# Seven block products in another order, with their weight sums spread over the row

## The chip, the core and the metric

One NeuronCore of a Trainium2 chip. TensorE (PE) multiplies into PSUM banks, VectorE (DVE) and ScalarE (ACT) work beside it, GpSimd (POOL) does next to nothing here, and SyncE (SP) issues the transfers from HBM. Each engine works through its own list of instructions in the order in which they stand, and engines wait for each other by semaphores. The metric is the time of one execution on the device in microseconds.

## The reference, cut to what matters

A decoder layer over 256 tokens of width 2048: a mixer (attention and a convolution), then a gated feed-forward of width 5632. The change lies in the feed-forward:

```python
h = rmsnorm(x, norm_pre_ffn[l])
g = jnp.einsum('bsd,df->bsf', h, w_gate[l])
up = jnp.einsum('bsd,df->bsf', h, w_up[l])
f = jnp.einsum('bsf,fd->bsd', jax.nn.silu(g) * up, w_down[l])
x = x + rmsnorm(f, norm_post_ffn[l])
```

## The kernel before, in words

**fp32 out of three products.** An fp32 operand is split into a rounded part h and a remainder l. A weight tile holds 4 x 128 rows and 512 columns (128 partitions x 2048 numbers, 1 MB). Its `split` is one cast on ScalarE (`wh`, L185 or L915) and one subtraction on VectorE (`wl`, L186 or L916). TensorE then makes 12 matmuls of 512 columns with it for 128 tokens: 8 with `wh`, then 4 with `wl`. These 12 matmuls are a **step**.

**A pair.** The 5632 columns are done 512 at a time, f = 0 to 10. For f = 1 to 10 the gate and the up product of one f are a `Pair`. With X = [X11 X12; X21 X22] (two token blocks, the upper half of the 2048 inputs in two blocks) and W = [r11 r12; r21 r22] (gate columns, up columns) the upper half of the inputs is done with seven block products, P1 to P7, in place of eight. The lower half is done plainly: g0 and g1 are its two gate tiles, u0 and u1 its two up tiles, each with a step for either token block (a and b). That makes 7 + 8 = 15 steps to a pair. P1, P2 and P3 take r11, r21 and r22 as they are; P5, P7, P6 and P4 take sums of weights: r11 becomes r12 - r11, r12 becomes r22 - r12, x becomes r22 - r11, and later x becomes r21 - x (`last_sum`). Each of these is one VectorE instruction over 128 x 2048 (L946). The left operands (`sumh`, `suml`) are sums of blocks of X, formed once by `form_sums`.

**What is collected.** P1, P6, P5 and P3 run in bank b1, P2, g0a and g1a in b2, P7, g0b, g1b and P4 in b7, u1b ends in b8. ScalarE copies b1 away after P1, P6 (`v`) and P5 (`s`, L1016); VectorE adds b7 to s (L1017, the "s add"). `gate(0)` after g1a and `gate(1)` after P4 add v to the bank on VectorE (L1000), then ScalarE takes the silu (L1001). `up(0)` after u0's and u1's steps for block a, and `up(1)` for block b (L1026 and L1005), multiply the two; then `act_put` has TensorE transpose the result (`ft`, eight matmuls), and ScalarE and VectorE split it (L208, L209). The buffers M that hold v, s and sg are three in turn, so the s of one pair is written where `up(1)` of the pair before has read.

**The order.** `steps` lists the steps of a pair; the u steps of a pair are put between the first steps of the next one (`fill`). `run_stream` goes through the list: after the last step of tile i it splits tile i + 4 and runs what hangs on that tile's `post`. Three buffers "w" take the loads; a load is issued when VectorE has read what the buffer held. Jobs that `spawn` puts aside run so many steps later. Each engine gets its instructions in the order in which the Python code makes them.

**The stages.** After f = 0 come parts of the feed-forward: f = 1, 2, then the down product; f = 3 to 5, down; 6 to 8, down; 9 and 10, down. A pair follows directly on another pair six times (f = 2, 4, 5, 7, 8, 10); I call that a **transition**, and count it from P7 of one pair to P7 of the next.

Of the kernel before, what the change touches and what calls it, by code (L numbers as in the profile page):

```python
# [25 lines left out]
F32 = mybir.dt.float32  # L26
# [5 lines left out]
P = 128  # L32
# [28 lines left out]
def hybrid_layer_kernel(ctx: ExitStack, tc: tile.TileContext, x, xt, pack, lamv,  # L61
# [664 lines left out]
    def form_sums():  # L726

        r = v3(T("sums"), 4)
        h, l = H2.part(1)
        for tb in range(2):  # L730
            tok = slice(tb * P, (tb + 1) * P)

            nc.vector.tensor_tensor(out=r[:, 2 * tb:2 * tb + 2].rearrange("p a (k t) -> p (a k) t", k=4),
                                    in0=h[:, :, tok].bitcast(F32), in1=l[:, :, tok].bitcast(F32),
                                    op=ALU.add)
        for o, a, b, op in [(3, 2, 3, ALU.add), (2, 0, 2, ALU.subtract), (0, 3, 0, ALU.subtract),
                            (1, 1, 0, ALU.subtract)]:
            nc.vector.tensor_tensor(out=r[:, o], in0=r[:, a], in1=r[:, b], op=op)
        sh, sl = v3(T("sumh", F32R), 4), v3(T("suml", F32R), 4)
        nc.scalar.copy(sh, r)  # L740
        nc.vector.tensor_tensor(out=sl, in0=r, in1=sh.bitcast(F32), op=ALU.subtract)
        st_["S"] = [t.rearrange("p s (k t) -> p s k t", k=4) for t in (sh, sl)]

    def residual(tb, bank):
        xr, mg = st_["x", tb], st_["mixg", tb]
        tok = slice(tb * P, (tb + 1) * P)
        square_into(bank, part[:, tb, 3:4])
        if tb:
            yield 1
        nc.vector.tensor_tensor(out=mg[:, 3 * C:], in0=bank, in1=st_["gpost"][:, 3 * C:],  # L750
                                op=ALU.mult)
        r = partial_rstd(part, tb, "rpost")

        def x2(n):
            c = slice(n * C, (n + 1) * C)
            nc.vector.scalar_tensor_tensor(out=xr[:, c], in0=mg[:, c], scalar=r[:, 0:1],
                                           in1=xr[:, c], op0=ALU.mult, op1=ALU.add)

        def tr(n):
            bk = aux_bank("ht")  # L760
            for j in range(4):
                nc.tensor.transpose(bk[:, j * P:(j + 1) * P],
                                    xr[:, n * C + j * P:n * C + (j + 1) * P], ident)
            for eng in range(2):
                for j in range(4):
                    k = n * 4 + j
                    g = pk[:, PK_GFFN + k:PK_GFFN + k + 1]
                    h, l = H2.at(k, 1, tok)
                    b = bk[:, j * P:(j + 1) * P]
                    if eng == 0:  # L770
                        nc.scalar.activation(h[:, 0], b, ACTF.Copy, scale=g)
                    else:
                        nc.vector.scalar_tensor_tensor(out=l[:, 0], in0=b, scalar=g,
                                                       in1=h[:, 0].bitcast(F32), op0=ALU.mult,
                                                       op1=ALU.subtract)

        x2(0)
        yield 1
        x2(1)
        x2(2)  # L780
        yield 1
        x2(3)
        tr(0)
        for n in range(1, 4):
            yield 1
            tr(n)
        yield 3
        for n in range(4):
            square_into(xr[:, n * C:(n + 1) * C], part2[:, tb, n:n + 1])
        yield 1  # L790
        rstd2[tb] = partial_rstd(part2, tb, "rffn")

        nc.sync.dma_start(xd[tb], xr)
        st_["x", tb] = None
        if tb:
            yield 2
            form_sums()

    oc = []
    need = {0: [lambda: st_["av", 0]], 4: [lambda: st_["av", 1]],  # L800
# [120 lines left out]
    class Pair:  # L921
# [5 lines left out]
        def __init__(self, f, A, k):  # L927
            self.f, self.A, self.k = f, A, k
            cols = [(f * C, C)]
            gt = [WTile(w_gate, 4 * i * P, SPLIT, cols) for i in range(4)]  # L930
            ut = [WTile(w_up, 4 * i * P, SPLIT, cols) for i in range(4)]
            self.g, self.u = gt[:2], ut[:2]
            self.r11, self.r21, self.r12, self.r22 = gt[2], gt[3], ut[2], ut[3]
            self.x = Slot()
            p = self.p = {
                1: Product(self, 1, self.r11, None, [("w", self.r11)]),
                7: Product(self, 7, self.r12, "r", [("r", self.r12), ("r", self.r22)]),
                6: Product(self, 6, self.x),
                5: Product(self, 5, self.r11, "w", [("w", self.x)]),
                2: Product(self, 2, self.r21, None, [("r", self.r21)]),  # L940
                3: Product(self, 3, self.r22, "r"),
                4: Product(self, 4, self.x, "w")}
            p[3].post = [self.last_sum]

        def sub(self, out, a, b):
            nc.vector.tensor_tensor(out=out.w, in0=a.w, in1=b.w, op=ALU.subtract)  # L946

        def sums(self):
            self.sub(self.r11, self.r12, self.r11)
            self.sub(self.r12, self.r22, self.r12)  # L950
            self.sub(self.x, self.r22, self.r11)

        def last_sum(self):
            self.sub(self.x, self.r21, self.x)
# [1 line left out]

        def steps(self, fill):

            fill[0][0][1].post = [self.sums]
            s = {n: [(self, t, n, 0)] for n, t in self.p.items()}  # L960
            g = [[(self, t, f"g{i}", tb) for tb in range(2)] for i, t in enumerate(self.g)]
            return (s[1] + fill[0] + s[7] + s[6] + fill[1] + s[5] + s[2] + g[0] + s[3] + g[1] + s[4])

        def up_steps(self):
            return [[(self, t, f"u{i}", tb) for tb in range(2)] for i, t in enumerate(self.u)]
# [1 line left out]
        def matmuls(self, t, what, tb):  # L967
            tok = [slice(0, P), slice(P, 2 * P)]
            if what == 1:
                self.b1 = mm_bank("b1")  # L970
            elif what == 2:
                self.b2 = mm_bank("b2")
            elif what == 7:
                self.b7 = ps.tile([P, 2, C], F32, tag="sc", bufs=1, name="b7")[:, 0]
            elif what == "u0" and tb == 1:
                self.b8 = mm_bank("b8")
            if what in (1, 2, 4):
# [20 lines left out]

        def gate(self, tb, bank, part):
            nc.vector.tensor_tensor(out=self.sg[:, tb], in0=bank, in1=part, op=ALU.add)  # L1000
            nc.scalar.activation(self.sg[:, tb], self.sg[:, tb], ACTF.Silu,  # L1001
                                 scale=rstd2[tb][:, 0:1])

# [4 lines left out]
        def after(self, what, tb):  # L1008
# [8 lines left out]
                nc.vector.tensor_tensor(out=self.s, in0=self.b7, in1=self.s, op=ALU.add)  # L1017
            elif what == "g1" and tb == 0:
                self.sg = v3(M("sg"), 2)
                self.gate(0, self.b2, self.v[:, 0])  # L1020
            elif what == 4:
                self.gate(1, self.b7, self.v[:, 1])
            elif what == "u1" and tb == 0:
                self.up(0, self.b1)
            elif what == "u1":
                nc.vector.tensor_tensor(out=self.s, in0=self.b8, in1=self.s, op=ALU.add)  # L1026
                self.up(1, self.s)
                st_["act", self.f] = spawn(act_put(self.A, self.k, self.sg), 2)

    def act_put(A, k, sg):  # L1030
        for tb in range(2):
# [138 lines left out]
```

## Time and profile before

| | |
|---|---|
| median of 3 runs | 1110.38 us (1110.32 to 1110.83) |
| the profiled execution's own time | 1110.2 us |
| its span, first to last instruction | 1108.4 us |
| PE busy | 1058.8 us (96%), 4766 matmuls |
| DVE busy | 821.9 us (74%), 858 instructions |
| ACT busy | 561.9 us (51%), 586 instructions |
| granted TensorE clock, mean | 0.990 of full speed |
| HBM | 208.99 MB read, 192 GB/s over the span |

The profiled execution lies 1.8 us above its span (launch and end) and 0.2 us below the median, so its own stretches can be used as they stand. Busy shares are means over stages of different kinds; what a stage waits for is read from that stage. A matmul is drawn to its modelled end, so that matmuls back to back overlap in the rows; the distance of their starts is what each costs.

### The profile page before, as it was taken

The page shows a single profiled execution, that of the slowest core. Times are in us where ns is not written, and L with a number is a line of the kernel's source. Part 1 is how long each engine was busy: PE and PEld are TensorE (multiplying, and loading weights), DVE is VectorE, ACT ScalarE, POOL GpSimd, SP SyncE. Part 2 cuts the span into 40 slices and gives each one's busy share as a digit, 9 for nine tenths or more (in the row PEclk, how much of TensorE's full clock was granted, in tenths as well). Part 3 has the DMA queues.
Part 4 walks back from the last instruction along what each step waited for, and adds up shares of the span by engine and source line. Part 5 has one row for each costly group of instructions (what it writes and reads, how often), then busy time and mean ns, then how long its engine had stood idle before and what let it go on. Part 6 is the DMA issues. An engine that isn't in the chain of part 4 may idle for free.

```text
span 1108.4 us, 12013 instructions
## 1 busy us (share of the span) xinstructions
PE 1058.8 (96%) x4766; PEld 864.7 (78%) x4766; DVE 821.9 (74%) x858; ACT 561.9 (51%) x586; POOL 10.8 (1%) x16
## 2 busy tenths in 40 slices
PE   9999999999999969899999989999999899999996
PEld 7778888788888857688887777888777788887785
DVE  6689999897557788864677867658787865777765
ACT  6754554655636553644454454435374543445541
POOL 0000000001000000000000000000000000000000
PEclk9999999999999989999999999999999999999998
DMA  9876545444848426377372826844553686372661
GB/s 311 302 254 208 190 152 190 152 154 150 304 158 297 153 81 223 114 268 272 106 237 88 283 77 201 299 145 148 193 196 108 214 284 224 88 254 86 243 241 76
DMA packets 114264, 213.97 MB, mean 193 GB/s; under 512 B 4088, under 2 KB 23840, under 8 KB 112928
## 3 DMA queue, kind: packets, MB, share of 16 engines
q1 hardware_dynamic: 114208, 213.21, 56.6%
q8 instruction: 37, 0.61, 0.2%
q14 instruction: 19, 0.16, 0.0%
HBM read 208.99 MB, written 4.21 MB: 192 GB/s over the span
## 4 chain that ended last, share of the span: by engine, by line
PE 63%; DVE 15%; DMA 8%; ACT 7%; issue 6%; POOL 1%; SPq 0%; DVEq 0%; POOLq 0%; ACTq 0%
PE mm L259 15%; PE mm L260 15%; PE mm L262 14%; PE b L993 10%; PE b L996 5%; DVE wl L186 5%; ACT wh L185 4%; DMA w<-in_w_up_dram 3%; DVE w L946 3%; DMA w<-in_w_gate_dram 2%; DVE raw L946 1%; ACT wh L915 1%; DMA w<-in_w_in_dram 1%; DVE wl L916 1%; DVE sg L1005 1%
## 5 line engine op out<-in xcount | busy, mean ns | idle before, releaser
L186 DVE TENSOR_TENSOR wl<-w,wh 128x2048 fp32r<-128x2048 f32 (+1 forms) x160 | 340.0, 2128 | 171.6 <-ACT wh L185 165.6
L185 ACT CAST wh<-w 128x2048 fp32r<-128x2048 f32 (+1 forms) x160 | 284.1, 1781 | 168.4 <-PE mm L260 80.6
L993 PE MATMUL b<-wh,h2h 128*128 128x512 f32 x440 | 172.9, 393 | 9.2 <-DVE s L1017 9.2
L996 PE MATMUL b<-wh,h2l 128*128 128x512 f32 x440 | 171.4, 390 | 0.0
L259 PE MATMUL mm<-wh,act 128*128 128x512 f32 x352 | 137.4, 390 | 0.2 <-ACT act L208 0.2
L260 PE MATMUL mm<-wh,act 128*128 128x512 f32 x352 | 137.1, 389 | 0.2 <-DVE act L209 0.2
L259 PE MATMUL mm<-wh,xh 128*128 128x512 f32 x320 | 127.8, 399 | 0.6 <-ACT wh L185 0.6
L260 PE MATMUL mm<-wh,xl 128*128 128x512 f32 x320 | 125.1, 391 | 0.0
L993 PE MATMUL b<-wl,h2h 128*128 128x512 f32 x440 | 117.7, 389 | 0.0
L916 DVE TENSOR_TENSOR wl<-w,wh 128x2048 fp32r<-128x2048 f32 x40 | 91.2, 2286 | 31.9 <-ACT wh L915 31.9
L993 PEld LDWEIGHTS b<-wh,h2h 128*128 128x128 f32 x440 | 82.6, 188 | 29.3 <-DVE s L1017 11.7
L993 PEld LDWEIGHTS b<-wl,h2h 128*128 128x128 f32 x440 | 82.6, 188 | 17.3
L996 PEld LDWEIGHTS b<-wh,h2l 128*128 128x128 f32 x440 | 82.7, 188 | 16.8
L915 ACT CAST wh<-w 128x2048 fp32r<-128x2048 f32 x40 | 76.4, 1909 | 35.6 <-PE mm L260 15.8
L262 PE MATMUL mm<-wl,act 128*128 128x512 f32 x352 | 94.2, 389 | 0.0
L442 DVE SCALAR_TENSOR_TENSOR conv_acc<-conv_in,pk,conv_acc 128x255 f32<-128x255 f32 (+14 forms) x240 | 94.1, 460 | 0.0
L262 PE MATMUL mm<-wl,xh 128*128 128x512 f32 x320 | 87.3, 391 | 0.2 <-DVE wl L186 0.2
L916 DVE TENSOR_TENSOR wl<-raw,wh 128x2048 fp32r<-128x2048 f32 x30 | 68.6, 2287 | 23.7 <-ACT wh L915 23.7
L993 PE MATMUL b<-wh,sumh 128*128 128x512 f32 x160 | 65.6, 410 | 18.8 <-DVE sg L1000 12.0
L260 PEld LDWEIGHTS mm<-wh,act 128*128 128x128 f32 x352 | 66.1, 188 | 14.1 <-DVE act L209 0.5
L259 PEld LDWEIGHTS mm<-wh,act 128*128 128x128 f32 x352 | 66.1, 188 | 14.1 <-ACT act L208 0.5
L262 PEld LDWEIGHTS mm<-wl,act 128*128 128x128 f32 x352 | 66.1, 188 | 13.7
(170 smaller groups left out, 1290.4 us busy)
## 6 DMA issues: line engine op xcount, KB each, us to landing
w<-in_w_down_dram SPq DMA_DIRECT2D x44, 1024.0 KB, 5.2
w<-in_w_gate_dram SPq DMA_DIRECT2D x34, 1024.0 KB, 5.3
w<-in_w_in_dram SPq DMA_DIRECT2D x24, 1024.0 KB, 5.1
w<-in_w_up_dram SPq DMA_DIRECT2D x24, 1024.0 KB, 5.3
raw<-in_w_up_dram SPq DMA_DIRECT2D x20, 1024.0 KB, 7.7
w<-in_w_out_dram SPq DMA_DIRECT2D x16, 1024.0 KB, 5.0
w<-in_w_in_dram SPq DMA_DIRECT2D x24, 512.0 KB, 5.0
raw<-in_w_gate_dram SPq DMA_DIRECT2D x10, 1024.0 KB, 7.7
```

The costliest lines, as they stand in the source:

```text
L185: nc.scalar.copy(self.h[:, a:b], self.w[:, a:b])
L186: nc.vector.tensor_tensor(out=self.l[:, a:b], in0=self.w[:, a:b], in1=self.h[:, a:b].bitcast(F32), op=ALU.subtract)
L259: nc.tensor.matmul(bank, lhsT=h, rhs=t.h[:, j], start=first, stop=False)
L260: nc.tensor.matmul(bank, lhsT=l, rhs=t.h[:, j], start=False, stop=False)
L262: nc.tensor.matmul(bank, lhsT=h, rhs=t.l[:, j], start=False, stop=last)
L442: return lambda: nc.vector.scalar_tensor_tensor(out=conv_acc[:, cb, s:], in0=conv_in[:, cb, :S - s], scalar=w, in1=conv_acc[:, cb, s:], op ...
L915: nc.scalar.copy(self.h, w)
L916: nc.vector.tensor_tensor(out=self.l, in0=w, in1=self.h.bitcast(F32), op=ALU.subtract)
L946: nc.vector.tensor_tensor(out=out.w, in0=a.w, in1=b.w, op=ALU.subtract)
L993: nc.tensor.matmul(bank, lhsT=h[:, j], rhs=rhs, start=start and pas == 0 and j == 0, stop=stop and pas == 1 and j == SPLIT - 1, skip_group ...
L996: nc.tensor.matmul(bank, lhsT=l[:, j], rhs=rhs, start=False, stop=False, skip_group_check=True)
L1005: nc.vector.scalar_tensor_tensor(out=self.sg[:, tb], in0=src, scalar=rstd2[tb][:, 0:1], in1=self.sg[:, tb], op0=ALU.mult, op1=ALU.mult)
```

## The change: what it does

- The order of a pair's last steps: P5, P2, g0, P3, g1, P4 becomes P5, P2, P3, g0, g1, P4.
- The three weight sums, made together before (after u0's split of the coming pair), are made one each after the splits of P1, u0 and P7.
- b7 was allocated anew for each pair in the first half of a two-bank tile. Now that tile is allocated once, and pairs use its halves in turn. The program as built still holds a wait of P7's first matmul for `gate(1)` of the pair before, though that reads the other half.
- The silu of `gate` is issued two steps after its addition, and `act_put` three steps after `up(1)` in place of two.
- `form_sums` is issued a step earlier, and its split (`split_sums`) two steps after that.

No instruction is added or left out.

```diff
@@ -736,6 +736,9 @@
         for o, a, b, op in [(3, 2, 3, ALU.add), (2, 0, 2, ALU.subtract), (0, 3, 0, ALU.subtract),
                             (1, 1, 0, ALU.subtract)]:
             nc.vector.tensor_tensor(out=r[:, o], in0=r[:, a], in1=r[:, b], op=op)
+        return r
+
+    def split_sums(r):
         sh, sl = v3(T("sumh", F32R), 4), v3(T("suml", F32R), 4)
         nc.scalar.copy(sh, r)
         nc.vector.tensor_tensor(out=sl, in0=r, in1=sh.bitcast(F32), op=ALU.subtract)
@@ -793,8 +796,10 @@
         nc.sync.dma_start(xd[tb], xr)
         st_["x", tb] = None
         if tb:
+            yield 1
+            r = form_sums()
             yield 2
-            form_sums()
+            split_sums(r)
 
     oc = []
     need = {0: [lambda: st_["av", 0]], 4: [lambda: st_["av", 1]],
@@ -940,15 +945,13 @@
                 2: Product(self, 2, self.r21, None, [("r", self.r21)]),
                 3: Product(self, 3, self.r22, "r"),
                 4: Product(self, 4, self.x, "w")}
+
+            p[1].post = [lambda: self.sub(self.r11, self.r12, self.r11)]
+            p[7].post = [lambda: self.sub(self.x, self.r22, self.r11)]
             p[3].post = [self.last_sum]
 
         def sub(self, out, a, b):
             nc.vector.tensor_tensor(out=out.w, in0=a.w, in1=b.w, op=ALU.subtract)
-
-        def sums(self):
-            self.sub(self.r11, self.r12, self.r11)
-            self.sub(self.r12, self.r22, self.r12)
-            self.sub(self.x, self.r22, self.r11)
 
         def last_sum(self):
             self.sub(self.x, self.r21, self.x)
@@ -956,10 +959,10 @@
 
         def steps(self, fill):
 
-            fill[0][0][1].post = [self.sums]
+            fill[0][0][1].post = [lambda: self.sub(self.r12, self.r22, self.r12)]
             s = {n: [(self, t, n, 0)] for n, t in self.p.items()}
             g = [[(self, t, f"g{i}", tb) for tb in range(2)] for i, t in enumerate(self.g)]
-            return (s[1] + fill[0] + s[7] + s[6] + fill[1] + s[5] + s[2] + g[0] + s[3] + g[1] + s[4])
+            return (s[1] + fill[0] + s[7] + s[6] + fill[1] + s[5] + s[2] + s[3] + g[0] + g[1] + s[4])
 
         def up_steps(self):
             return [[(self, t, f"u{i}", tb) for tb in range(2)] for i, t in enumerate(self.u)]
@@ -971,7 +974,10 @@
             elif what == 2:
                 self.b2 = mm_bank("b2")
             elif what == 7:
-                self.b7 = ps.tile([P, 2, C], F32, tag="sc", bufs=1, name="b7")[:, 0]
+
+                if "b7" not in st_:
+                    st_["b7"] = ps.tile([P, 2, C], F32, tag="sc", bufs=1, name="b7")
+                self.b7 = st_["b7"][:, self.f % 2]
             elif what == "u0" and tb == 1:
                 self.b8 = mm_bank("b8")
             if what in (1, 2, 4):
@@ -998,6 +1004,7 @@
 
         def gate(self, tb, bank, part):
             nc.vector.tensor_tensor(out=self.sg[:, tb], in0=bank, in1=part, op=ALU.add)
+            yield 2
             nc.scalar.activation(self.sg[:, tb], self.sg[:, tb], ACTF.Silu,
                                  scale=rstd2[tb][:, 0:1])
 
@@ -1017,15 +1024,15 @@
                 nc.vector.tensor_tensor(out=self.s, in0=self.b7, in1=self.s, op=ALU.add)
             elif what == "g1" and tb == 0:
                 self.sg = v3(M("sg"), 2)
-                self.gate(0, self.b2, self.v[:, 0])
+                spawn(self.gate(0, self.b2, self.v[:, 0])).run()
             elif what == 4:
-                self.gate(1, self.b7, self.v[:, 1])
+                spawn(self.gate(1, self.b7, self.v[:, 1])).run()
             elif what == "u1" and tb == 0:
                 self.up(0, self.b1)
             elif what == "u1":
                 nc.vector.tensor_tensor(out=self.s, in0=self.b8, in1=self.s, op=ALU.add)
                 self.up(1, self.s)
-                st_["act", self.f] = spawn(act_put(self.A, self.k, self.sg), 2)
+                st_["act", self.f] = spawn(act_put(self.A, self.k, self.sg), 3)
 
     def act_put(A, k, sg):
         for tb in range(2):
```

How it moves instructions, at three places. **VectorE in a transition, the later half** (f = 7 to f = 8), from the split of u1 to the s add. `wl` with L186 are splits of u1 and g0 (g1 has its own further on), `wl` with L916 or L921 those of products, `w<-raw,w` is `last_sum`, the three rows with sg and s are `up(0)` and `up(1)`. Before:

```order
L186 TENSOR_TENSOR wl<-w,wh 128x2048
L916 TENSOR_TENSOR wl<-w,wh 128x2048
L916 TENSOR_TENSOR wl<-raw,wh 128x2048
L186 TENSOR_TENSOR wl<-w,wh 128x2048
L1005 SCALAR_TENSOR_TENSOR sg<-b_5527,rffn_2927,sg 128x512
L1026 TENSOR_TENSOR s<-b_5838,s 128x512
L1005 SCALAR_TENSOR_TENSOR sg<-s,rffn_3054,sg 128x512
L916 TENSOR_TENSOR wl<-raw,wh 128x2048
L946 TENSOR_TENSOR w<-raw,w 128x2048
L1017 TENSOR_TENSOR s<-b_5857,s 128x512
```

These are the splits of u1, P5, P2 and g0, the two ups, the split of P3, `last_sum`, the s add. And now:

```order
L186 TENSOR_TENSOR wl<-w,wh 128x2048
L921 TENSOR_TENSOR wl<-w,wh 128x2048
L921 TENSOR_TENSOR wl<-raw,wh 128x2048 x2
L954 TENSOR_TENSOR w<-raw,w 128x2048
L1012 SCALAR_TENSOR_TENSOR sg<-b_5521,rffn_2927,sg 128x512
L1033 TENSOR_TENSOR s<-b_5832,s 128x512
L1012 SCALAR_TENSOR_TENSOR sg<-s,rffn_3053,sg 128x512
L186 TENSOR_TENSOR wl<-w,wh 128x2048
L1024 TENSOR_TENSOR s<-b_3158,s 128x512
```

The split of P3 and `last_sum` have moved ahead of the ups, and the split of g0 behind them.

**VectorE in a transition, the earlier half** (same pair), from P1's split to `gate(1)`. Rows L946 or L954 are the weight sums, L1000 or L1006 the gates. Before (the first row holds the splits of P4 and P1):

```order
L916 TENSOR_TENSOR wl<-w,wh 128x2048 x2
L186 TENSOR_TENSOR wl<-w,wh 128x2048
L946 TENSOR_TENSOR w<-raw,w 128x2048
L946 TENSOR_TENSOR raw<-raw 128x2048
L946 TENSOR_TENSOR w<-raw,w 128x2048
L1000 TENSOR_TENSOR sg<-b_5672,v 128x512
L916 TENSOR_TENSOR wl<-raw,wh 128x2048
L1000 TENSOR_TENSOR sg<-b_5579,v 128x512
```

And now:

```order
L921 TENSOR_TENSOR wl<-w,wh 128x2048
L954 TENSOR_TENSOR w<-raw,w 128x2048
L186 TENSOR_TENSOR wl<-w,wh 128x2048
L954 TENSOR_TENSOR raw<-raw 128x2048
L1006 TENSOR_TENSOR sg<-b_5666,v 128x512
L921 TENSOR_TENSOR wl<-raw,wh 128x2048
L954 TENSOR_TENSOR w<-raw,w 128x2048
L1006 TENSOR_TENSOR sg<-b_3158,v 128x512
```

One sum stands behind the split of P1, one behind that of u0, and the third between P7's split and `gate(1)`. On ScalarE the silu of `gate(0)` stood ahead of P7's cast and that of `gate(1)` ahead of P6's; each now stands behind it.

**VectorE ahead of the first pair** (f = 1), from P1's split on. L733 and L738 form the sums of X blocks, L741 or L744 is their remainder `suml`, prt and rs belong to the norm that the first silu needs. Before:

```order
L916 TENSOR_TENSOR wl<-w,wh 128x2048
L186 TENSOR_TENSOR wl<-w,wh 128x2048
L946 TENSOR_TENSOR w<-raw,w 128x2048
L946 TENSOR_TENSOR raw<-raw 128x2048
L946 TENSOR_TENSOR w<-raw,w 128x2048
L688 TENSOR_REDUCE prt<-part_90 128x1
L101 TENSOR_SCALAR rs<-prt 128x1
L916 TENSOR_TENSOR wl<-raw,wh 128x2048
L733 TENSOR_TENSOR sums<-h2h_2787,h2l_2788 128x1024 x2
L738 TENSOR_TENSOR sums<-sums 128x512 x4
L741 TENSOR_TENSOR suml<-sums,sumh 128x2048
L916 TENSOR_TENSOR wl<-w,wh 128x2048
```

And now:

```order
L921 TENSOR_TENSOR wl<-w,wh 128x2048
L954 TENSOR_TENSOR w<-raw,w 128x2048
L186 TENSOR_TENSOR wl<-w,wh 128x2048
L954 TENSOR_TENSOR raw<-raw 128x2048
L688 TENSOR_REDUCE prt<-part_90 128x1
L101 TENSOR_SCALAR rs<-prt 128x1
L921 TENSOR_TENSOR wl<-raw,wh 128x2048
L954 TENSOR_TENSOR w<-raw,w 128x2048
L733 TENSOR_TENSOR sums<-h2h_2787,h2l_2788 128x1024 x2
L738 TENSOR_TENSOR sums<-sums 128x512 x4
L921 TENSOR_TENSOR wl<-w,wh 128x2048
L744 TENSOR_TENSOR suml<-sums,sumh 128x2048
```

The first sum of weights stands behind P1's split, prt and rs a sum earlier, and P6's split ahead of `suml`.

## Rows read from the trace of the kernel before

**Rows 1.** Who PE waited for: us in total, times, longest

```profile
PE b L993 <- DVE sg L1000: 12.0, 6, 2.9
PE b L993 <- DVE s L1017: 9.2, 6, 1.5
PE b L993 <- ACT sumh L740: 6.8, 1, 6.8
PE ft L1034 <- DVE sg L1005: 5.9, 10, 0.8
PE b L996 <- DVE suml L741: 1.5, 1, 1.5
```

**Rows 2.** Groups of PE by line: busy, mean ns | idle before

```profile
L996 PE MATMUL b<-wh,h2l 128*128 128x512 f32 x440 | 171.4, 390 | 0.0
...
L1034 PE MATMUL ft<-ident,sg 128*128 128x128 f32 x80 | 11.8, 278 | 6.0 <-DVE sg L1005 5.9
```

**Rows 3.** Stretches: length, busy PE, PEld, DVE, ACT, POOL, clock, DMA, GB/s

```profile
599.26:647.93 48.67, 44.15 (x189) 35.62 (x189) 38.56 (x23) 24.25 (x19) 0.00 (x0) 0.96 0.51 173
803.48:851.53 48.05, 42.98 (x189) 34.22 (x189) 38.56 (x23) 24.27 (x19) 0.00 (x0) 1.00 0.51 175
...
600.64:604.05 3.41, 3.41 (x10) 2.65 (x9) 2.36 (x2) 3.41 (x4) 0.00 (x0) 0.50 0.00 0
...
398.00:402.60 4.60, 3.19 (x8) 2.51 (x9) 4.60 (x3) 4.60 (x4) 0.00 (x0) 0.50 0.00 0
```

**Rows 4.** VectorE in order of time, transition 803 to 851: start, us, [idle before]

```profile
805.93 2.29 DVE L916 TENSOR_TENSOR wl<-w,wh 128x2048 fp32r<-128x2048 f32 x1 [2.59 <-ACT wh L915]
...
817.67 2.29 DVE L186 TENSOR_TENSOR wl<-w,wh 128x2048 fp32r<-128x2048 f32 x1 [2.76 <-PE b L993]
...
821.25 0.75 DVE L1005 SCALAR_TENSOR_TENSOR sg<-s,rffn,sg 128x512 f32<-128x512 f32 x1
...
836.27 2.29 DVE L186 TENSOR_TENSOR wl<-w,wh 128x2048 fp32r<-128x2048 f32 x1 [1.47 <-ACT wh L185]
...
845.22 0.68 DVE L1000 TENSOR_TENSOR sg<-b,v 128x512 f32<-128x512 f32 x1
848.49 2.29 DVE L916 TENSOR_TENSOR wl<-raw,wh 128x2048 fp32r<-128x2048 f32 x1 [2.59 <-ACT wh L915]
850.70 0.68 DVE L1000 TENSOR_TENSOR sg<-b,v 128x512 f32<-128x512 f32 x1
```

**Rows 5.** ScalarE in order of time, the same transition

```profile
815.73 1.91 ACT L185 CAST wh<-w 128x2048 fp32r<-128x2048 f32 x1 [3.45 <-DMA w<-in_w_gate_dram]
...
822.09 0.59 ACT L1016 COPY s<-b 128x512 f32<-128x512 f32 x1 [2.65 <-DVE sg L1005]
...
846.56 1.90 ACT L915 CAST wh<-raw 128x2048 fp32r<-128x2048 f32 x1
```

**Rows 6.** The chain that ended last, same transition: start, us, what

```profile
814.01 1.13 PE b L993 x5
...
816.73 0.92 PE b L993 x4
...
829.24 4.99 DMA w<-in_w_up_dram
```

**Rows 7.** VectorE in order of time, ahead of the first pair

```profile
375.18 2.29 DVE L186 TENSOR_TENSOR wl<-w,wh 128x2048 fp32r<-128x2048 f32 x1 [1.88 <-ACT wh L185]
...
387.63 2.29 DVE L916 TENSOR_TENSOR wl<-raw,wh 128x2048 fp32r<-128x2048 f32 x1 [3.17 <-ACT wh L915]
389.84 2.35 DVE L733 TENSOR_TENSOR sums<-h2h,h2l 128x1024 f32<-128x1024 f32 x2
392.23 2.87 DVE L738 TENSOR_TENSOR sums<-sums 128x512 f32<-128x512 f32 x4
397.06 2.29 DVE L741 TENSOR_TENSOR suml<-sums,sumh 128x2048 fp32r<-128x2048 f32 x1 [1.96 <-ACT sumh L740]
```

**Rows 8.** ScalarE in order of time, the same place

```profile
385.12 0.69 ACT L823 ACTIVATE sg<-mm,rffn 128x512 f32<-128x512 f32 x1 [6.93 <-POOL rffn L102]
```

## The prediction, made before the changed kernel was run

> **What bounds the kernel now.** The table shows PE busy 96% of the span, so the first view is who PE waited for. Five lines make 35.4 us, all in the feed-forward's pairs [rows 1]: P7 on `gate(1)` (12.0 us, six times), g0b on the s add (9.2, six times), the transposes on the ups (5.9), and once, before the first pair, P7 on the sums of X (6.8 and 1.5). Six is the number of transitions; pairs that follow a down stage do not wait. A wait is longer than its line says: a matmul is drawn 0.39 us long [rows 2], but twelve of them take 2.72 us (the last four of a step start at 814.01 and at 816.73 in the next) [rows 6], 0.227 each, so each gap loses 0.16 us more.
>
> The second view is the stretch of a transition [rows 3]: 48.67 and 48.05 us. PE's own need in it is 15 steps of 2.72 and eight transposes (11.8 us over 80, so 1.2) [rows 2, 6]: 42.0 us. VectorE is busy 38.56 of it. So neither engine fills it, and the third view, VectorE in order of time, shows why: it stands still 2.59, 2.76, 1.47 and 2.59 us [rows 4], and 38.56 + 9.41 = 47.97 is the transition. A ring through VectorE sets its length, and PE waits on the ring:
> - 2.59 us twice. `gate(0)` is done at 845.9, ScalarE must first take its silu, and casts P7's weights from 846.56 to 848.46 only [rows 5]; VectorE, whose next row is P7's split, waits. The same with `gate(1)`, its silu and P6.
> - 2.76 us. VectorE reaches g0's split early, but its load lands late: ScalarE's cast waited for the transfer until 815.73 and ended at 817.64 [rows 5] (the row names PE, but the split starts as the cast ends). The ups are queued behind and end at 822.00, where P5 had ended at 817.65 (816.73 + 0.92) [rows 4, 6]. ScalarE's copy of s waits 2.65 us for them [rows 5], since s takes the buffer that up(1) reads; then come P3's split, `last_sum` and only then the s add that g0b waits for.
> - 1.47 us, the same with u0's load.
>
> **The change, part by part.** No work is added: the same 38.56 us of VectorE and 42.0 us of PE. What it moves is where VectorE stands still. I write the new queue down by hand, counted from the start of P5 in a transition, with 2.21 us for a split or sum (starts of back to back rows: 848.49 and 850.70) [rows 4], 1.9 for a cast, 5.1 for a load (4.99 in the chain) [rows 5, 6], 0.6 to 0.75 for the rest. On PE, P3 starts at 5.4, the transposes at 8.2, g0b at 12.1; P4 ends at 23.0, P7 of the next pair starts at 31.1, all again after 42.0.
>
> VectorE, with up(1) ending at 3.5 (the last entry shows from where): g0 split to 5.7, s add 6.3, g1 8.5, P4 10.7, act 12.0. P1's buffer is free at 5.7, its load lands at 10.8, the cast ends at 12.7; here 0.7 us are idle. P1 14.9, r11 17.1, u0 19.3 (loaded since about 13.6), r12 21.6, `gate(0)` 22.2. P7's cast follows r12 at once, the silu now being behind it, and ends at 23.4: idle 1.2. P7 25.7, x 27.9, `gate(1)` 28.5. P6's cast ends at 29.8: idle 1.2. P6 32.0; ScalarE then v 30.3, cast of u1 32.1, silu 32.8, cast of P5 34.6; u1 34.3, P5 36.8, P2 39.0, P3 41.2, `last_sum` 43.4, ups 45.5, which is 42.0 + 3.5. The ring closes: 38.56 + 0.7 + 1.2 + 1.2 = 41.7, just under PE's 42.0. g0's load (from 34.3) now lands at 39.4 and waits for VectorE, not VectorE for it.
>
> So, step by step:
> - **P3 ahead of g0.** The s add (6.3) is 5.8 us early for g0b. Price: 9.2 + 6 x 0.16 = **10.2 us** gone. P3 now follows P5 with one step between, and its bank b1 must have been copied to s by then: the copy ends 0.6 after up(1), 4.1 against 5.4. This is the smallest slack, 1.3 us.
> - **Sums spread, silu later, two banks.** `gate(1)` at 28.5 is 2.6 us early for P7. 12.0 + 6 x 0.16 = **13.0 us** gone. After two of these waits the granted clock stood at 0.50 for 3.41 us (the stretch from 600.64; one like it at 648.4) [rows 3]. That is 1.2 GHz, so half of each was lost: **3.4 us**. The two banks alone buy nothing: the built program's P7 waits for `gate(1)` as before. What gains is that `gate(1)` comes sooner.
> - **act_put one step later.** Transposes at 8.2, ups at 3.5: 5.9 + 6 x 0.16 = **6.9 us** gone. At the end of a part they stand one step closer to the down product that reads them: ScalarE's and VectorE's two rows each (1.1 + 1.3 us) fit in the step of 2.72 that is left, and in the last part they cannot move (the next step needs them). I count nothing.
> - **Sums of X.** Today's order is u1's split at 375.18, three weight sums, P7's split at 387.63 after 3.17 us idle, then L733 at 389.84, 5.3 us of sums, the cast (1.96), `suml` to 399.35 [rows 7]. That idle comes of the silu at 385.12, which waited for the norm behind all three sums [rows 8]. Now the first sum fills the 1.88 us ahead of u1's split; two sums, prt and rs are done at 380.3, the silu at 381.6, the cast 383.5, P7's split 385.7, x 387.95. The sums end at 393.2, `sumh` at 395.1, P6's split, now ahead, at 395.4, and `suml` at 397.7 against 399.35: **1.7 us**. The rest of this wait stays, and so does the half clock behind it (0.50 in 398 to 402.6) [rows 3]. Bounds: nothing, if P6's cast or a load comes late; at most the 6.8 + 1.5 of the two lines and some 1.7 for the clock, 10.0.
>
> The trace shows no row of the new order, so each price is bounded by nothing below and its own wait above, except that new waits can appear; the worst of them is a rival below. Loads took 5.0 in this chain, and 1.5 more at P1 would lengthen the ring to 43.2, 1.2 over PE: at most 6 x 1.2 = 7 us back. Sum: 10.2 + 13.0 + 3.4 + 6.9 + 1.7 = 35.2. Against the profiled execution's own 1110.2 (0.2 below the median) that is **1075 us**.
>
> **The rivals.**
> - *P7 goes on waiting.* The program's wait is not removed, and `gate(1)` now has six rows of 2.21 us from P1's split ahead of it. If it comes 2.6 us later than in my queue, P7 waits again; at worst all 13.0 and 3.4 stay: 1075 + 16.4 = 1091. For it: the six rows. Against: two idle times of 2.59 shrink to 1.2, and P1's split and r11 can start before u0's load, which now holds up all three sums. The Trainium skill, Perfetto Trace Analysis, Optimizing Tensor Performance (Matmuls), says that groups which rotate through different banks let the collecting of one overlap the matmuls of the next; by that alone this wait would go however late `gate(1)` is, and the time would be 1075 here too. No row shows it yet, and the wait in the program speaks against it.
> - *P3 takes over the wait.* If up(1) ends where it does today, 4.35 us after P5's end, the copy ends at 5.0 and P3, 2.72 after P5, waits 2.3: six times 13.8, so 1089. For it: the copy's 2.65 us [rows 5]. Against: g0's split, whose load held the ups, is behind them now.
> - *Slower.* The splits of P3 and `last_sum`, 4.4 us, now stand ahead of the ups. If the front of VectorE's queue stays as late as today, up(1) ends 8.75 after P5, the copy 9.4, and P3 waits 6.7 us: six times 40, and 1110 - 35 + 40 = 1115. It decides from 35.2 / 6 = 5.9 us a transition, that is up(1) 7.9 us after P5's end. The Trainium skill, TensorE: Matmul & The Clock Gate, Architectural detail, has ScalarE and VectorE as strict queues and matmuls in program order, which is the rule by which this would happen; the trace agrees, the copy and P7's split waiting behind rows that they do not need. Against: nothing ahead of the ups waits for a late load any more.
>
> **How the numbers follow.** Forecast 0.70 (1068 to 1084, by the bounds of the sums of X and of the loads), P7 waiting 0.10, P3 waiting 0.13, slower 0.05, and 0.02 for no change within 0.2% (2.2 us, what a measurement here can tell). The range, 1067 to 1090, takes in the forecast's own and most of the two middle cases. Faster 0.93, same 0.02, slower 0.05.
>
> **What would show it.** In the changed kernel's waits the lines of `gate(1)`, the s add and the ups are gone or under 1 us each; a line of P3's b matmuls on ScalarE's s would be the second and third rival, of P7 on the gate the first. A transition is 42 to 43 us long, with VectorE idle under 4 us in it. ScalarE's g0 cast no longer waits for a transfer. The clock is 1.00 in every transition. P7 of the first pair starts its second matmul near 397.7. I would be wrong if ring and PE, 0.3 us apart, both stretch: then each transition waits a little everywhere.

## The result, and the profile after

The changed kernel takes **1080.65 us** (1080.08 to 1080.68, four runs) against 1110.61 us of the kernel before in the same comparison (1110.32 to 1111.69): a ratio of 0.9727, 95% interval 0.971 to 0.9744. Forecast were 1075.0 us and a range of 1067 to 1090. The profiled execution took 1080.65 us too, with a span of 1078.9.

TensorE is now busy nearly all the time, and the chain that ended last runs through it (first line: busy time and share of the span; second: shares of the chain by engine):

```profile
PE 1052.6 (98%) x4766; PEld 866.3 (80%) x4766; DVE 823.2 (76%) x858; ACT 562.4 (52%) x586; POOL 10.8 (1%) x16
...
PE 84%; DVE 8%; ACT 3%; DMA 2%; issue 2%; POOL 1%; SPq 0%; DVEq 0%; POOLq 0%; ACTq 0%
```

Who PE waited for, the answer to [rows 1]:

```profile
PE b L999 <- ACT sumh L743: 4.8, 1, 4.8
PE mm L259 <- ACT act L208: 2.5, 1, 2.5
PE b L1002 <- DVE suml L744: 1.9, 1, 1.9
PE mm L260 <- DVE act L209: 1.6, 1, 1.6
PE b L999 <- ACT s L1023: 1.5, 2, 0.8
```

The lines of `gate(1)` (12.0), of the s add (9.2) and of the ups (5.9) are gone. The wait for the sums of X is there still, 6.7 us in place of 8.3. Two lines are new: P3 waits twice for the copy s, and the down product of the last part waits once for ScalarE's and once for VectorE's rows of act.

The transitions that answer to [rows 3], from P7 to P7, and the stretch of the new waits:

```profile
590.96:632.80 41.84, 41.84 (x190) 34.56 (x188) 38.50 (x23) 23.32 (x18) 0.00 (x0) 1.00 0.57 201
782.53:824.42 41.89, 41.89 (x190) 34.54 (x188) 38.51 (x23) 23.29 (x18) 0.00 (x0) 1.00 0.56 201
...
1028.11:1035.00 6.89, 5.25 (x12) 3.80 (x13) 2.99 (x3) 0.43 (x1) 0.00 (x0) 0.53 0.61 209
```

48.67 and 48.05 us have become 41.84 and 41.89, at the full clock, and PE is busy in all of it; VectorE's work is the same 38.5 us. These two (f = 4 to 5 and 7 to 8) are the only transitions with another transition just ahead of them, and they hold the transposes as well. The other four start at the first pair of a part: three took 42.3 to 43.2 us and take 40.80 now, which is PE's 15 steps of 2.72; the first, with the wait for the sums of X in it, took 47.3 and takes 46.3. The third row is the loss that is new: the clock is 0.53 of full speed on the mean there, so nearly all of it at the lower level of 1.2 GHz.

VectorE in the later of these transitions, the answer to [rows 4]:

```profile
780.32 0.68 DVE L1006 TENSOR_TENSOR sg<-b,v 128x512 f32<-128x512 f32 x1
...
793.79 2.29 DVE L954 TENSOR_TENSOR w<-raw,w 128x2048 f32<-128x2048 f32 x1
796.00 0.74 DVE L1012 SCALAR_TENSOR_TENSOR sg<-b,rffn,sg 128x512 f32<-128x512 f32 x1
...
798.04 2.29 DVE L186 TENSOR_TENSOR wl<-w,wh 128x2048 fp32r<-128x2048 f32 x1
...
807.69 2.29 DVE L921 TENSOR_TENSOR wl<-w,wh 128x2048 fp32r<-128x2048 f32 x1 [1.16 <-ACT wh L920]
...
816.63 0.69 DVE L1006 TENSOR_TENSOR sg<-b,v 128x512 f32<-128x512 f32 x1
818.77 2.29 DVE L921 TENSOR_TENSOR wl<-raw,wh 128x2048 fp32r<-128x2048 f32 x1 [1.46 <-ACT wh L920]
...
823.18 0.69 DVE L1006 TENSOR_TENSOR sg<-b,v 128x512 f32<-128x512 f32 x1
```

`last_sum`, the ups and g0's split stand back to back (793.79, 796.00, 798.04), where VectorE stood still 2.76 us for g0. It waits 1.16 us for P1's cast and 1.46 for P7's, where 0.7 and 1.2 were worked out.

The first and the last row are `gate(1)` of two pairs in a row, so their distance is one turn of VectorE: 42.86 us (42.73 between f = 4 and 5), and not the 41.7 worked out. That is longer than PE's 41.89. PE does not feel it at P7, because P7 started 1.5 us after `gate(1)` had ended at 782.53 and 0.6 us after it at 824.42: a lead left from the pair before is used up, and a part ends before it is gone. P3's two waits on s, 0.7 and 0.8 us, fall in the pairs that follow (f = 5 and f = 8). What more pairs in a row would do, no run shows.

### The profile page after: what moved, and what is told of

Its sections match the earlier page's. It is cut to its first block, busy times and chain, and to the rows that moved or that the text cites. A ratio compares the mean times of both kernels' runs of the same rounds, so it can differ in the third digit from the quotient of the medians.

```text
span 1078.9 us, 12015 instructions
## 1 busy us (share of the span) xinstructions
PE 1052.6 (98%) x4766; PEld 866.3 (80%) x4766; DVE 823.2 (76%) x858; ACT 562.4 (52%) x586; POOL 10.8 (1%) x16
## 4 chain that ended last, share of the span: by engine, by line
PE 84%; DVE 8%; ACT 3%; DMA 2%; issue 2%; POOL 1%; SPq 0%; DVEq 0%; POOLq 0%; ACTq 0%
PE b L999 23%; PE mm L259 15%; PE mm L260 15%; PE mm L262 15%; PE b L1002 11%; DVE wl L186 2%; DVE wl L921 2%; ACT wh L185 2%; DMA w<-in_w_in_dram 1%; DVE w L954 1%; PE ft L1041 1%; DVE conv_acc L442 1%; DMA rb<-in_rel_bias_dram 1%; ACT wh L920 1%; PE scmm L262 1%
## 5 line engine op out<-in xcount | busy, mean ns | idle before, releaser
L186 DVE TENSOR_TENSOR wl<-w,wh 128x2048 fp32r<-128x2048 f32 (+1 forms) x160 | 340.6, 2130 | 130.4 <-ACT wh L185 126.8
L921 DVE TENSOR_TENSOR wl<-w,wh 128x2048 fp32r<-128x2048 f32 x40 | 91.6, 2289 | 38.1 <-ACT wh L920 37.3
L921 DVE TENSOR_TENSOR wl<-raw,wh 128x2048 fp32r<-128x2048 f32 x30 | 68.2, 2290 | 26.0 <-ACT wh L920 26.0
L920 ACT CAST wh<-raw 128x2048 fp32r<-128x2048 f32 x30 | 57.4, 1913 | 50.6 <-DVE raw L954 45.9
```

The lines of the kernel that those rows point to most:

```text
L186: nc.vector.tensor_tensor(out=self.l[:, a:b], in0=self.w[:, a:b], in1=self.h[:, a:b].bitcast(F32), op=ALU.subtract)
L920: nc.scalar.copy(self.h, w)
L921: nc.vector.tensor_tensor(out=self.l, in0=w, in1=self.h.bitcast(F32), op=ALU.subtract)
```

## The experiments

Each edit is against the changed kernel unless it says before. Each was timed against the kernel before on the same chip (1110.3 to 1111.3 us there).

**One bank for b7.**

```diff
-                if "b7" not in st_:
-                    st_["b7"] = ps.tile([P, 2, C], F32, tag="sc", bufs=1, name="b7")
-                self.b7 = st_["b7"][:, self.f % 2]
+                self.b7 = ps.tile([P, 2, C], F32, tag="sc", bufs=1, name="b7")[:, 0]
```

> The changed kernel with b7 allocated anew for each pair in the first half, as before. Theory (the two banks buy nothing, since the built program's P7 waits for gate(1) either way and gate(1) now comes early): 1080.7 us, within 1 us of the changed kernel, and no line of P7 on the gate among PE's waits. Rival (the banks took the wait of P7 away): the 13.0 us of that wait and 3.4 us of half clock come back, 1097 us.

Measured: 1080.74 us (ratio 0.9731, 0.9716 to 0.9745); P7 waits nowhere for the gate. The two banks do nothing. Nor do they hold the wait off where `gate(1)` is late: in the next run, which has both, P7 waits for the gate twice, 1.1 us together. The Trainium skill, Perfetto Trace Analysis, Optimizing Tensor Performance (Matmuls), advises to rotate matmul groups through different banks so that collecting one overlaps the next. These runs do not show that gain: with both banks P7 still waited for `gate(1)` of the pair before, which reads the other one, because the program as built holds that wait. Whether banks whose waits follow the turns would gain, no run shows.

**The silu issued at once.**

```diff
         def gate(self, tb, bank, part):
             nc.vector.tensor_tensor(out=self.sg[:, tb], in0=bank, in1=part, op=ALU.add)
-            yield 2
             nc.scalar.activation(self.sg[:, tb], self.sg[:, tb], ACTF.Silu,
...
```

The two callers change with it, from `spawn(self.gate(...)).run()` to `self.gate(...)`.

> The changed kernel with the silu issued right behind its addition. Theory (VectorE, ScalarE and the loads make a ring that is just as long as PE's work in a transition): the casts of P7 and P6 stand behind a silu of 0.69 us each and behind gate(0) and gate(1), 1.3 to 1.4 us later each; the ring grows by some 2.7 us, six times, less what PE has to spare: 1090 to 1097 us, and VectorE's idle time ahead of those two splits grows from 1.45 to about 2.6 us. Rival (the sums and the order alone gave the ring room): within 2 us of 1080.7.

Measured: 1094.66 us (0.9853, 0.9839 to 0.9868), 14 us more than the changed kernel. VectorE ahead of the splits of P7 and P6, in the transition from f = 4 to f = 5:

```profile
631.26 2.29 DVE L921 TENSOR_TENSOR wl<-raw,wh 128x2048 fp32r<-128x2048 f32 x1 [2.59 <-ACT wh L920]
...
638.95 2.29 DVE L921 TENSOR_TENSOR wl<-w,wh 128x2048 fp32r<-128x2048 f32 x1 [2.59 <-ACT wh L920]
```

The 2.59 us of [rows 4] are back, to the digit. PE feels them at another line, though, as it would if VectorE's lateness is handed on to whatever PE needs next from it. Here that is the copy that stands behind the ups, and a transition is 44.7 us (f = 4 to 5). The second line is the down product's wait in the last part, 2.5 us in the changed kernel:

```profile
PE b L999 <- ACT s L1022: 10.5, 6, 2.0
...
PE mm L259 <- ACT act L208: 3.9, 1, 3.9
```

**g0 ahead of P3 again.**

```diff
-            return (... + s[5] + s[2] + s[3] + g[0] + g[1] + s[4])
+            return (... + s[5] + s[2] + g[0] + s[3] + g[1] + s[4])
```

> The changed kernel with g0 ahead of P3 again, all else kept. Theory (P3 ahead of g0 keeps VectorE busy while g0's load comes): in the changed kernel VectorE was free for the next row at 642.72, and the cast of g0, which waited for its load, ended at 646.33. With g0 next, VectorE stands still there for some 3.6 us a transition, and the ups are queued behind: 2.5 to 3.6 us of it reach PE, six times, 1096 to 1102 us, with waits of PE on s or on the ups. Rival (the order only brought the s add forward, which the shorter ring does by itself): 1081 to 1083 us.

Measured: 1093.07 us (0.9839, 0.9818 to 0.986), so 12.4 us more; the theory's place is right, its price 3 us too high. VectorE waits for g0's cast 2.99 us, not 3.6, and PE waits for the s add as in [rows 1]:

```profile
PE b L999 <- DVE s L1024: 9.9, 6, 2.6
```

**act_put two steps after up(1).**

```diff
-                st_["act", self.f] = spawn(act_put(self.A, self.k, self.sg), 3)
+                st_["act", self.f] = spawn(act_put(self.A, self.k, self.sg), 2)
```

> The changed kernel with act_put two steps after up(1) again, for all pairs. Theory (three steps put the rows of act behind the preparation of the next tile in the last part, which costs 2.47 + 1.65 us of waiting and 1.5 to 2 us of half clock; the ups now end by the end of the P2 step, so that the transposes need not wait): 1074 to 1076 us, faster than both kernels. Rival (the wait of the transposes on the ups, 5.9 us before, comes back): 1080.7 - 5.4 + 6.9 = 1082 us.

Measured: **1072.98 us** (0.966, 0.9643 to 0.9676), 7.7 us less than the changed kernel and 1 us below the theory's range. PE waits for the ups 0.4 us in all, and P3 no longer waits for s: the eight transposes now stand ahead of it. A transition is 41.73 us, all of it PE:

```profile
590.57:632.30 41.73, 41.73 (x190) 34.46 (x188) 38.41 (x23) 22.43 (x18) 0.00 (x0) 1.00 0.57 201
```

What it gains lies at the last part. ScalarE there in the changed kernel:

```profile
1025.67 1.90 ACT L185 CAST wh<-w 128x2048 fp32r<-128x2048 f32 x1 [5.26 <-PE ft L1041]
1027.48 1.07 ACT L208 CAST act<-ft 128x512 fp32r<-128x512 f32 x2
```

VectorE behind it:

```profile
1027.60 2.29 DVE L186 TENSOR_TENSOR wl<-w,wh 128x2048 fp32r<-128x2048 f32 x1 [4.57 <-ACT wh L185]
1029.81 1.28 DVE L209 TENSOR_TENSOR act<-ft,act 128x512 fp32r<-128x512 f32 x2
```

And ScalarE with two steps:

```profile
1023.35 1.07 ACT L208 CAST act<-ft 128x512 fp32r<-128x512 f32 x2 [4.83 <-PE ft L1041]
1024.31 1.92 ACT L185 CAST wh<-w 128x2048 fp32r<-128x2048 f32 x1
```

With three steps the job of the last pair isn't due when the down product wants its rows. The code then runs it on the spot, behind the preparation of a further tile, whose cast (1.90) and split (2.29) PE has to sit through. With two steps it is due before, and the rows act stand ahead of the cast. By the code, only the last part is hit because it has two pairs and not three, so its down product comes to the last pair's rows two steps sooner. From the last P7 to the end of the span it is 104.6 us (974.26 to 1078.9) with three steps and 98.4 (972.82 to 1071.2) with two: 6.3 of the 7.7 us. 0.4 us lie between the first P7 and the last, and 1.0 ahead of the first (395.95 against 394.95), where the two kernels don't differ.

**The three weight sums together.**

```diff
-            p[1].post = [lambda: self.sub(self.r11, self.r12, self.r11)]
-            p[7].post = [lambda: self.sub(self.x, self.r22, self.r11)]
...
-            fill[0][0][1].post = [lambda: self.sub(self.r12, self.r22, self.r12)]
+            fill[0][0][1].post = [self.sums]
```

> The changed kernel with the three weight sums together again behind u0's split, all else kept. Theory (the spread by itself is worth nothing in a transition): with the sums together VectorE waits some 1.8 us for u0's cast, since r11 no longer fills that time, but the 1.45 and 1.46 us ahead of P7's and P6's splits go, since their casts then run beside a sum; the ring gets no longer. Ahead of the first pair r11 no longer fills the wait for u1's cast, up to 1.9 us. 1079 to 1083 us, no line of P7 on the gate. Rival (the spread is what makes gate(1) early): P7 waits for the gate again, at least half of the 13.0 us of before: 1087 us or more.

Measured: 1080.14 us (0.9725, 0.9709 to 0.9741). In the transitions the spread is worth nothing, rather less: the two long ones take 41.73 us without it, and P3 never waits for s. Ahead of the first pair it is worth about what the prediction's X term said: P7 waits 6.8 us for `sumh` in place of 4.8.

**Before, with P3 ahead of g0 alone.**

```diff
-            return (... + s[2] + g[0] + s[3] + g[1] + s[4])
+            return (... + s[2] + s[3] + g[0] + g[1] + s[4])
```

> The kernel before with P3 ahead of g0 and nothing else. Theory (one ring through VectorE sets all of PE's waits): the 2.76 us that VectorE waited for g0's cast are filled, the ring falls from 48.05 to some 45.2 us against 42.0 us of PE, so 6 x 2.8 = 17 us go: 1094 us, and the waits that are left (on the gate, or on s and the ups) add up to some 6 x 3.2 = 19 us. Rival (each wait is an own loss, as the sum of the prediction counts them): only the s add's 10.2 us go, 1100 us, and P7's 12.0 us on the gate and the transposes' 5.9 us stay as they were.

Measured: 1088.83 us (0.9807, 0.9792 to 0.9821), 21.4 us less than before. Of the waits of [rows 1] all three shrank, not the s add's alone:

```profile
PE b L993 <- DVE sg L1000: 4.7, 4, 2.0
PE ft L1034 <- DVE sg L1005: 3.5, 5, 0.7
```

The transition from f = 4 to f = 5, P7 to P7, in its windows:

```profile
594.39:639.79 45.40, 42.67 (x188) 34.40 (x189) 38.58 (x23) 24.19 (x19) 0.00 (x0) 1.00 0.52 185
```

It is 45.40 us long, where 45.2 was worked out from the ring; the one from f = 7 to f = 8 is 45.39. The rival, that each wait is a loss of its own, is out, since the waits that the edit does not touch shrank too. The theory's totals were off as well: the time is 5 us below its 1094, and these two lines make 8.2 us where it had some 19 left. One of the two stretches at half clock of [rows 3] went, which is at most 1.7 us of it; the rest was not traced.

**Before, with the silu later alone.**

```diff
             nc.vector.tensor_tensor(out=self.sg[:, tb], in0=bank, in1=part, op=ALU.add)
+            yield 2
             nc.scalar.activation(self.sg[:, tb], self.sg[:, tb], ACTF.Silu,
...
```

The two callers change as in the whole change.

> The kernel before with the silu two steps later and nothing else. Theory (one ring): the two idle times of 2.59 us ahead of P7's and P6's splits fall to 1.3 each, the ring to some 45.5 us: 6 x 2.6 = 15.5 us go, 1095 us, up to 3.4 less if the half clock goes with them; all three waits of PE (gate, s add, ups) shrink together. Rival (each wait is an own loss): gate(1) comes 1.3 us earlier, 6 x 1.3 = 8 us of P7's wait go, the s add's 9.2 and the ups' 5.9 us stay: 1103 us.

Measured: **1080.44 us** (0.973, 0.9715 to 0.9744): this one edit gives what the whole change gives. It gained 29.8 us, where the theory said 15.5, or 18.9 with the half clock. VectorE at the place of [rows 4]:

```profile
825.60 0.68 DVE L1000 TENSOR_TENSOR sg<-b,v 128x512 f32<-128x512 f32 x1
826.20 2.28 DVE L916 TENSOR_TENSOR wl<-raw,wh 128x2048 fp32r<-128x2048 f32 x1
828.40 0.69 DVE L1000 TENSOR_TENSOR sg<-b,v 128x512 f32<-128x512 f32 x1
829.00 2.28 DVE L916 TENSOR_TENSOR wl<-w,wh 128x2048 fp32r<-128x2048 f32 x1
```

Both idle times of 2.59 us are gone, not halved: with the sums together x is ready before P7's split, so ScalarE casts P7 beside a sum and P6 beside a split. In the changed kernel x stands behind P7's split, and each cast must wait for its sum, which is the 1.46 us seen above. Transitions are 43.34 and 41.73 us; 4.6 us of waiting for the s add are left, and no line of P7 for the gate above 0.2 us. All three waits shrank together, as the theory said and the rival did not.

**Before, with act_put three steps later alone.**

```diff
-                st_["act", self.f] = spawn(act_put(self.A, self.k, self.sg), 2)
+                st_["act", self.f] = spawn(act_put(self.A, self.k, self.sg), 3)
```

> The kernel before with act_put three steps after up(1) and nothing else. Theory (one ring through VectorE sets the length of a transition, and PE's wait for the ups is only where a part of that falls): PE runs one step further before the transposes and waits the longer for the s add, which VectorE reaches no sooner; the 5.9 us are not gained, and the last part loses its 2.5 + 1.7 us and the half clock behind, 5 to 6 us: 1115 to 1117 us, slower than before. Rival (an own term, as the prediction's sum has it): 6.9 us are gained and 5 to 6 lost in the last part, 1109 us.

Measured: 1125.23 us (four runs, 1119.11 to 1125.32; ratio 1.0111, 1.0082 to 1.014): slower, and by more than either said. PE's waits in the pairs:

```profile
PE b L993 <- DVE s L1017: 17.4, 6, 4.3
PE b L993 <- DVE sg L1000: 8.1, 5, 2.4
```

They make 25.5 us, where the three lines of [rows 1] made 12.0 + 9.2 + 5.9 = 27.1. So the wait for the ups was not taken away but joined to that for the s add. The length of a long transition stays near the 48.67 and 48.05 us of before, now 48.39 and 48.50, though some of it is at half clock. First, the transition from f = 4 to f = 5; second, one of the six places where PE waits for the s add:

```profile
602.06:650.45 48.39, 45.43 (x188) 36.83 (x189) 38.62 (x23) 24.24 (x19) 0.00 (x0) 0.93 0.49 174
675.36:680.64 5.28, 5.28 (x12) 4.12 (x13) 5.28 (x4) 3.74 (x4) 0.00 (x0) 0.50 0.33 93
```

PE had stood 4.28 us ahead of 675.36, and the whole step that followed ran at 0.50, which is 1.2 GHz. Span and mean clock of this kernel:

```profile
core 0: 1123.6 us, clock 0.976
```

Most of the loss lies in the last part. The two profiles differ by 15.1 us: 1.3 ahead of the first P7, 4.4 from there to the last P7 (398.38 to 1011.88), and 9.4 behind it, where the down product now waits 3.6 + 1.9 us for act, at half clock behind the first of these waits. The mean clock fell from 0.990 to 0.976 of full speed, by estimate 0.014 x 1124 = 16 us at most, since PE stood still in part of that time. The waits by themselves make some 5 us more in the last part (the kernel before waits 0.4 us there) and 1.6 less in the pairs. That leaves some 11 us of the 15.1, most of it the clock by that estimate.

**form_sums ahead of P7's split.** On the changed kernel with act_put at two steps.

```diff
         if tb:
-            yield 1
             r = form_sums()
-            yield 2
+            yield 1
             split_sums(r)
```

> The changed kernel with act_put two steps after up(1) for all pairs, and form_sums issued as soon as the norm of the second token block is done, its split one step later. VectorE stood still there for 3.18 us ahead of P7's split. Theory (the wait of the first pair's P7 is the place of the sums of X in VectorE's row, not their length): sumh is cast from 385.3 in place of 393.0, P7 finds it ready at 390; suml comes 0 to 1.8 us late. Of the 4.99 + 2.25 us lost there and some 2.4 us of half clock behind, all but 2 go: 1063 to 1067 us. Rival (P7's split, 5 us later behind the sums, and x with P6's cast take over the wait): 1070 to 1073 us.

Measured: **1065.2 us** (0.9592, 0.9578 to 0.9607), the fastest of all, 7.8 us less than with act_put alone. VectorE ahead of the first pair in the changed kernel, the answer to [rows 7]:

```profile
384.30 2.29 DVE L921 TENSOR_TENSOR wl<-raw,wh 128x2048 fp32r<-128x2048 f32 x1 [3.17 <-ACT wh L920]
386.51 2.29 DVE L954 TENSOR_TENSOR w<-raw,w 128x2048 f32<-128x2048 f32 x1
388.71 2.35 DVE L733 TENSOR_TENSOR sums<-h2h,h2l 128x1024 f32<-128x1024 f32 x2
```

And with this edit:

```profile
380.73 2.35 DVE L733 TENSOR_TENSOR sums<-h2h,h2l 128x1024 f32<-128x1024 f32 x2
383.12 2.87 DVE L738 TENSOR_TENSOR sums<-sums 128x512 f32<-128x512 f32 x4
385.91 2.28 DVE L920 TENSOR_TENSOR wl<-raw,wh 128x2048 fp32r<-128x2048 f32 x1
```

The stretch from P7's first matmul on, in its windows:

```profile
390.64:400.00 9.36, 7.74 (x34) 6.08 (x33) 9.36 (x5) 9.36 (x7) 0.00 (x0) 1.00 0.19 49
```

The sums fill the 3.17 us in which VectorE waited for P7's cast. PE waits 1.6 us for `suml` in place of 4.8 + 1.7, and the half clock behind it is gone (1.00).

**The two small edits on the kernel before.** The silu two steps later, and form_sums as in the experiment ahead of this one; nothing else.

> The kernel before with two edits: the silu two steps later (1080.4 us by itself) and form_sums as soon as the norm of the second token block is done, its split one step later; the order of steps, the weight sums together and act_put two steps later stay. Theory: PE's wait of 6.6 + 1.5 us ahead of the first pair and 2.4 us of half clock behind it shrink as they did in the changed kernel, by some 6 of 10.5 us since the three sums still stand together ahead of it and VectorE's wait of 1.9 us for u1's cast stays: 1072 to 1076 us, with 4 to 5 us of waits for the s add left that P3 ahead of g0 would take away. Rival (the casts of P7 and P6 take over the wait there): 1079 to 1081 us.

Measured: 1075.49 us (0.9683, 0.9669 to 0.9698), with 4.5 us of waits for the s add, 1.2 for `sumh` and 2.0 for `suml` left. This run and the one ahead of it both land in the range that was worked out from the rows.

## Why the prediction was right, and where it was 5.6 us off

**The mechanism held.** A ring through VectorE, ScalarE and the loads was longer than PE's work, and the change makes it shorter, by 5 to 6 us. A long transition is 41.84 us of PE's own work, where 42.0 was worked out. The ring itself was put too short: VectorE's turn takes 42.7 to 42.9 us, not 41.7, so it did not come to lie under PE's work. The total hardly shows it, because a part has at most three pairs and the lead of 1.5 us lasts that long. From the first P7 to the last it is 578.3 us (395.95 to 974.26) where it was 609.1 (397.08 to 1006.15), 30.8 less; what lies behind the last P7, where the last s add and the last ups fall, went from 102.3 to 98.4 us with act_put at two steps, 3.9 less. Together 34.7 us, where the terms of the transitions made 33.5 (10.2 + 13.0 + 3.4 + 6.9). The 3.9 are of another kernel than the 30.8; the changed kernel itself loses 2.3 us behind its last P7, and why is said below.

**P3 ahead of g0** (10.2) and **silu later** (in the 13.0 + 3.4) are both real: without the one the changed kernel loses 12.4 us, without the other 14.0. But they are not two terms of a sum. Alone on the kernel before they give 21.4 and 29.8, which is 51 in sum, where the changed kernel with act_put at two steps is 38.3 us faster in all; both shorten one ring, and below 41.73 us a transition has nothing more to gain, since PE then runs without a pause. The bookkeeping by PE's lines got the total nearly right because the lines together are all the time that PE stood still in the pairs, whichever line a part of it is charged to, and nearly all of it went. As the price of a single edit they do not hold.

**"Sums spread, silu later, two banks"** stood as one step. Its gain is the silu's alone. The banks are worth nothing, as said, and so is the spread in a transition: it fills the wait for u0's cast, and opens 1.46 us each ahead of P7 and P6.

**Sums of X**: 1.7 forecast. The two gaps made 6.96 + 2.10 us of PE's time before and make 4.99 + 2.24 now, 1.8 less. Undone, the spread gives 2.0 of P7's wait back, so it is, as far as this shows, r11 in the wait for u1's cast that gains it. The second matmul of that P7 starts at 398.43, where 397.7 was forecast. That form_sums and its split stand apart was not tried by itself.

**The step that failed** is act_put one step later, **6.9 us gone**, with its last sentence: "At the end of a part they stand one step closer to the down product [...] and in the last part they cannot move (the next step needs them). I count nothing." They do move there, behind the cast and the split of another tile: 2.47 + 1.65 us of waiting and the half clock behind, 6.3 us by the ends of the two profiles. And the 6.9 us were not act_put's to give: with two steps the changed kernel waits 0.4 us for the ups, and three steps on the kernel before gain none of it. 1075 and that 6.3 make 1081.3, against 1080.65 measured; that the term of 6.9 did no harm to the sum is luck of the bookkeeping, since those waits went with the ring.

**The rivals.** P7 goes on waiting: no. P3 takes over the wait: a little, 1.5 us in two places, each in the last pair of a part of three. The slack was 1.3 us there by hand, but at f = 5 up(1) ended 5.6 us after P5's start and not 3.5, which fits a ring longer than worked out. Slower by a late front of VectorE's queue: no. That ScalarE's cast of g0 would no longer wait for its load was half right: at 644.42 it waits 2.04 us for the transfer, but VectorE has `last_sum` to do meanwhile.

## What to carry to other kernels

When several waits of the busiest engine all trace back to one other engine's queue, measure the length of a whole turn through that queue and compare it with the busy engine's own work; what an edit is worth is how much it shortens the turn, down to that floor, and not the line of waits that it seems to remove. Measure the turn on the slower queue itself afterwards: the busy engine can look free of waits while it uses up a lead. The cheapest way to shorten it is to look for a row that nobody needs soon standing ahead of one that the ring waits for (here a silu of 0.7 us ahead of a cast, or a cast of a later tile ahead of act), and to fill each idle time with rows that are ready, as form_sums was. A delay that is counted in steps has to be followed to the last turn of the loop, where the job isn't due in time and is run wherever the code stands.

## What was not expected

**Where several waits became one, the lower clock mostly followed.** Before, a wait of 0.28 and 0.82 us ahead of the transposes and one of 1.5 for the s add left the clock at 1.00 in the transition at 462 to 470. With act_put at three steps PE waited there once, for 3.24 us, and the next 3.1 us ran at 0.50; at 675.36 it was once for 4.28, with the same that follows. Behind the six waits for the s add the lower clock shows five times with three steps, and never before. In most of these places PE also waited longer in total, so the two are not separated; the clearest is the last, where 1.89 us in one piece (at 1035.52) was followed by 0.52, and 2.68 us in three pieces in the kernel before by 1.00. Nor does the length of a wait decide alone: behind 3.07 us at 880.16 the clock stayed at 1.00.
